# Column sums later on PE, a head split on Vector, 0/1 expert sums in FP32R, and expert weights in 8 KB blocks

## The chip, the cores and the metric

One core of one Trainium2 chip runs the whole program in one launch. The metric is device time in microseconds of one execution. A core has the engines PE (TensorE: matmuls, with weight loads listed as PEld), DVE (VectorE, called Vector here), ACT (ScalarE), POOL (GpSimd) and SP (SyncE, which issues most DMAs). Each engine works through its own instructions in order; semaphores tie them together. Sixteen DMA engines move data between HBM and SBUF.

## The reference

Two transformer blocks on 1024 tokens of width 1024, fp32.

```python
# first block: gated linear attention, then a mixture of experts
x = x + gla_mixer(rmsnorm(x, attn_norm), ...)          # 4 heads, dk 128, dv 256, chunks of 64
h = rmsnorm(x, ffn_norm)
x = rmsnorm(x + hier_moe(h, ...), final_norm)          # 8 groups x 8 experts, top 2 in one group
# an expert: (silu(h @ w1[e]) * (h @ w3[e])) @ w2[e], times the token's gate; summed per token
# second block
mod = silu(c) @ w_ada + b_ada                          # 1 x 1024 by 1024 x 6144, then six parts
...                                                    # SSD + local attention, then a conv FFN
```

w1 and w3 are 1024 x 256 and w2 is 256 x 1024 for each of 64 experts: 3.15 MB an expert, 201 MB in all.

## The kernel before

**First part (phase_gla).** Matmuls of fp32 accuracy are made of three FP32R matmuls: `split_w` (L194) turns a raw weight into a high part (ACT, L135) and a low part (a subtract, L136, on the engine it is given: GpSimd with `G_`, else Vector). For each head, `prep` (L449) projects q, k and two halves of r on PE (`projT`, L309 to L311), yielding after each group of three matmuls. Beside the two r projections it steps `along` (L332), a chain on Vector and ACT that makes the gates and the scaled operands and ends with L391. It also splits the weights needed next; the last, at step 8 of the second r projection, is the second half of the v weight. Then `projV_tile` (L251, L258 to L260) makes v tile by tile, and `core` (L395) does the attention of a head in 128 tokens: matmuls A (L403, L404), a masked copy AT on Vector (L409), matmuls on it (L418 to L421). The code's order is the order on each engine; nothing reorders it.

**Modulation beside it.** `modulation` (L474) is a generator that is stepped by `mod_step` at every second yield of prep(0), prep(1) and prep(2), and at every fourth of head 1's v projection; what is left is drained after prep(2). w_ada comes in 96 chunks of 128 x 512, 12 groups of 8, into six buffers. Vector multiplies each chunk by its scalar and adds it into one of two accumulators (L502, L504). When chunk 1 of the next group has been issued, the group's columns are summed over partitions on PE by `total` (L489): four matmuls of one column (L492), whose result Vector copies to mT at once (L509). At the end mT is turned on PE and stored.

**Expert stage (phase_moe).** Experts are worked through in 32 pairs, expert 2p in PE's columns 0 to 63, expert 2p+1 in 64 to 127; up to 64 slots per expert. Seven weight slots hold w13 (w1 beside w3, 2 MB) and w2 (1 MB) of experts loaded ahead; SP issues a load when the slot's earlier user is done. `load_13` (L920) writes a block of w1 as eight pieces of 1 KB per partition, with w3's pieces between them. A pair on PE, in order of issue:

- `down_t` (L996): the hidden values of the pair before are turned (mhd), Vector copies them (hidT).
- `slots_in` (L1183): the group's tokens are brought into slots by 0/1 matmuls in bf16 (L1189, L1194), ACT copies (xT).
- `rows_out` (L1208): the outputs of two pairs before are brought back to token rows, 160 to a group: y times the gate matrix wT in fp32, rows 0 to 127 in two matmuls of 512 columns (L1220), rows 128 to 159 in four of 256 columns side by side (L1224). ACT copies or Vector adds them (L1216) into Y0 and Y1, which are stored after each fourth pair.
- `hidden` (L980): x times w1 and w3, 16 fp32 matmuls of 512 columns (L986), two at a time; ACT's silu (L990) and Vector's product (L992).
- `turned` (L1199): the gate matrix of the pair is turned (mwt) and copied by ACT. `masks` (L1168): Vector makes the 0/1 and gate matrices of the next pair (L1177 to L1180).
- `down` (L1005): hidden values of the pair before times w2 (L1014), two halves of 512 columns; ACT copies one half to y (tile my), Vector the other (L1016).

Three PSUM buffers (mpy) go round between `down` and `rows_out`. GpSimd issues the gathers of the groups' tokens and the first loads of experts 5 and 6.

Of the kernel before, what the change touches and what calls it, by code (L numbers as in the profile page):

```python
# [70 lines left out]
class Slots:  # L71
# [78 lines left out]
def phase_gla(k, x, attn_norm, w_in, w_gate, b_gate, out_norm, w_o, ffn_norm, w_group, w_expert,  # L150
# [9 lines left out]
    with top:  # L160
# [312 lines left out]

        def modulation():  # L474
# [36 lines left out]
            yield  # L511
            ps = total(11)
# [400 lines left out]
def expert_loads(k, w1, w3, w2):  # L913

    nc = k.nc

    def row(w, e):
        return w[e] if isinstance(e, int) else w[bass.ds(e, 1)].rearrange("o a b -> (o a) b")

    def load_13(e, w, parts=1, eng=(nc.sync, nc.sync)):  # L920
        n = 8 // parts
        for k0 in range(0, 8, n):
            for c, src in enumerate((w1, w3)):
                eng[c].dma_start(out=w[:, k0:k0 + n, c * 256:c * 256 + 256],  # L924
                                 in_=row(src, e).rearrange("(p k) f -> p k f", k=8)[:, k0:k0 + n, :])

    def load_2(e, w, eng=nc.sync):
        eng.dma_start(out=w, in_=row(w2, e).rearrange("(p k) d -> p k d", k=2))

    return load_13, load_2  # L930


def phase_moe(k, h2_d, x1_d, y_d, keep, slots, load_13, load_2, w0):
# [3 lines left out]
    with ExitStack() as ctx:  # L937
# [24 lines left out]

        for name, n in (("my", D), ("MwT", GCAP)):
            sp.tile([128, n], F32, name=name)
        xa, xb = slots.xg, sp.tile([64, D], F32, name="xg1")
# [14 lines left out]
        def hidden(xT, *ws):  # L980
# [3 lines left out]
            for kk in range(8):  # L984
                for c, w in enumerate(ws):
                    nc.tensor.matmul(h[c * 64:c * 64 + 64, :], xT[:, kk, c * 64:c * 64 + 64], w[:, kk, :],  # L986
                                     start=(kk == 0), stop=(kk == 7), skip_group_check=True)

# [15 lines left out]

        def down(hT, *ws):  # L1005

            n = 64 * len(ws)
            y = sp.tile([128, D], F32, name="my")
            for half, copy in ((0, S.copy), (1, V.tensor_copy)):
                cs = slice(half * 512, half * 512 + 512)  # L1010
                ps = pyp.tile([128, 512], F32, name="mpy", tag="mpy")
                for kk in range(2):
                    for c, w in enumerate(ws):
                        nc.tensor.matmul(ps[c * 64:c * 64 + 64, :], hT[:, kk, c * 64:c * 64 + 64], w[:, kk, cs],  # L1014
                                         start=(kk == 0), stop=(kk == 1), skip_group_check=True)
                copy(y[0:n, cs], ps[0:n])  # L1016
                yield y[0:n]

        NP = 32
# [13 lines left out]
        with tc.If(most > GCAP), ExitStack() as over:  # L1033
# [85 lines left out]
            wa, wb = slots.w13(6), slots.w2(6)  # L1119
            x = ov.tile([64, D], F32, name="ox")  # L1120
            V.memset(x, 0.0)
            for j in range(NB):
# [5 lines left out]
                for half in range(2):  # L1128
# [4 lines left out]
                    S.copy(out=xT[:, half * 4:half * 4 + 4, 0:64], in_=ps[:, :, 0:64])  # L1133
                y = list(down(down_t(hidden(xT, wa)), wb))[-1]

# [9 lines left out]
        pb = yp.tile([96, D], BF16, name="xp1")  # L1145
        Y0, Y1 = yp.tile([128, D], F32, name="Y0"), yp.tile([128, 256], F32, name="Y1")

# [14 lines left out]
        def write_group(g):  # L1162
            r = g * GCAP
            for cs in (slice(0, D),) if g < 7 else (slice(0, 512), slice(512, D)):
                S.dma_start(out=y_d[r:r + 128, cs], in_=Y0[:, cs])
            S.dma_start(out=y_d[r + 128:r + GCAP, :].rearrange("t (h c) -> h t c", h=4), in_=Y1)

# [31 lines left out]
        def turned(w):  # L1199
# [43 lines left out]
        for p in range(NP):  # L1243
# [3 lines left out]
            if p > 1:  # L1247
                rows_out(p - 2, wT.pop(p - 2), ys.pop(p - 2))
            if p % 4 == 3 and p // 4 + 1 < 8:
# [11 lines left out]
            if p:  # L1261
                d = down(hT, *pair(w2, p - 1))
                ys[p - 1] = next(d)
# [1386 lines left out]
```

## Time and profile before

| what | us |
|---|---|
| median of 3 runs (lowest, highest) | 2372.03 (2367.1, 2373.81) |
| the profiled execution | 2370.45 |
| its span, first to last instruction | 2368.5 |
| PE busy (share of the span) | 2235.8 (94%) |
| DVE, ACT, POOL busy | 1376.2, 859.9, 569.1 |
| DMA | 408.61 MB, mean 173 GB/s |

Times in the trace are microseconds from the span's start. In the table by stage a row gives the stretch and its length, then the busy microseconds (x instructions) of PE, PEld, DVE, ACT and POOL, then the clock granted to TensorE (1.00 is 2.4 GHz, 0.50 is 1.2 GHz, values between are a mean of the two), the mean busy share of the 16 DMA engines (over 1 where packets overlap), and GB/s. In a timeline a row is one instruction or several alike merged: start, length, engine, line, operation, output<-input, shape, count, and in brackets the idle time before it and what ended it. A PE matmul in fp32 shows as two instructions; a matmul's length includes its way through the array, so the pace is read from start to start.

### The profile page before, as it was taken

What the parts mean: (1) busy time and instruction counts of PE and PEld (TensorE: products, weight loads), DVE (VectorE), ACT (ScalarE), POOL (GpSimd) and SP (SyncE); (2) the same over time, 40 slices, a digit from 0 to 9 for tenths busy, and PEclk for the clock granted to TensorE, in tenths of its full rate; (3) what the DMA queues carried; (4) which work ended last, traced back from release to release, by engine and by line L of the source; (5) the groups of instructions that cost most, each with busy time, mean ns of one, the idle gap of its engine ahead of it and who ended that gap; (6) DMA issues with size and microseconds to landing.
All of it is one profiled execution on the core that took longest, in us unless ns stands there. A gap on an engine that the chain in (4) does not pass through costs nothing.

```text
span 2368.5 us, 31053 instructions
## 1 busy us (share of the span) xinstructions
PE 2235.8 (94%) x11879; PEld 1609.8 (68%) x11879; DVE 1376.2 (58%) x2378; ACT 859.9 (36%) x1610; POOL 569.1 (24%) x520
## 2 busy tenths in 40 slices
PE   8899999996999999998999999999979999999996
PEld 7778888873444444434766788777768888887884
DVE  4766524564443333325355524666588888878988
ACT  4342434311222222214443334424444444444443
POOL 3222223201111111005300100346443333310036
PEclk9999999996999999997999999999989999999999
DMA  5544211648999999997511022444432222227442
GB/s 175 180 123 140 90 33 31 241 179 302 382 395 384 378 374 397 389 395 209 144 39 30 10 43 58 147 99 134 160 98 81 81 81 84 84 91 293 132 138 80
DMA packets 325054, 408.61 MB, mean 173 GB/s; under 512 B 43016, under 2 KB 264312, under 8 KB 316704
## 3 DMA queue, kind: packets, MB, share of 16 engines
q1 hardware_dynamic: 312064, 368.23, 45.9%
q0 software_dynamic: 4944, 18.37, 2.7%
q10 hardware_dynamic: 7888, 19.93, 2.2%
q8 instruction: 96, 1.57, 0.3%
q14 instruction: 62, 0.51, 0.1%
HBM read 360.29 MB, written 46.19 MB: 172 GB/s over the span
## 4 chain that ended last, share of the span: by engine, by line
PE 57%; DVE 5%; DMA 5%; SPq 3%; issue 3%; POOL 2%; ACT 2%; POOLq 0%; DVEq 0%; ACTq 0%
PE mh L986 8%; PE pu L2208 5%; PE pu L2211 5%; PE pu L2210 5%; PE mpy L1014 4%; PE pj L1356 2%; PE pj L1354 2%; PE pj L1352 2%; SPq L924 2%; PE pu L2389 2%; PE mpy L1220 2%; PE pu L2390 2%; PE pu L2387 2%; DMA w<-in_moe_w_dram 2%; PE mtr L1189 1%
## 5 line engine op out<-in xcount | busy, mean ns | idle before, releaser
L986 PE MATMUL mh<-w,xT 128*64 128x512 f32 x880 | 233.4, 598 | 5.7 <-DMA w<-in_moe_w_dram 5.1
L136 POOL TENSOR_TENSOR whl<-wraw,whl 128x1024 fp32r<-128x1024 f32 x35 | 87.1, 2494 | 327.7 <-ACT whl L135 186.5
L986 PEld LDWEIGHTS mh<-w,xT 128*64 128x64 f32 x880 | 76.0, 137 | 123.7 <-issue 108.9
L992 DVE TENSOR_TENSOR hid<-hid,mh 128x256 f32<-128x256 f32 x32 | 13.5, 421 | 220.5 <-ACT hid L990 220.5
L1014 PE MATMUL mpy<-w,hidT 128*64 128x512 f32 x512 | 117.1, 599 | 0.0
L1159 POOL TENSOR_TENSOR xg<-xg,xp 32x1024 f32<-32x1024 f32 x7 | 20.3, 2904 | 372.1 <-ACT xp L1155 372.1
L309 PE MATMUL pj<-hT,whl 128*128 128x512 f32 x256 | 105.4, 412 | 0.7 <-ACT rT L447 0.7
L1356 PE MATMUL pj<-hT,whl 128*128 128x512 f32 x256 | 102.9, 402 | 0.5 <-POOL whl L136 0.5
L1354 PE MATMUL pj<-hT,whl 128*128 128x512 f32 x256 | 103.0, 402 | 0.0
L1352 PE MATMUL pj<-hT,whl 128*128 128x512 f32 x256 | 102.3, 400 | 0.0
L990 ACT ACTIVATE hid<-mh 128x256 f32<-128x256 f32 x32 | 19.8, 619 | 223.9 <-PE mh L986 223.9
L311 PE MATMUL pj<-hT,whl 128*128 128x512 f32 x256 | 100.7, 394 | 0.0
L310 PE MATMUL pj<-hT,whl 128*128 128x512 f32 x256 | 100.5, 393 | 0.0
L2096 POOL TENSOR_TENSOR gr<-wraw,gr 128x512 f32<-128x512 f32 x30 | 58.0, 1932 | 164.2 <-DVE wup L136 59.1
L258 PE MATMUL pj<-whl,hT 128*128 128x256 f32 x256 | 82.5, 322 | 0.6 <-ACT hT L135 0.4
L2217 DVE TENSOR_TENSOR fup<-pu,fup 128x512 f32<-128x512 f32 x100 | 68.6, 686 | 23.0 <-PE pu L2211 23.0
L2389 PE MATMUL pu<-wup 128*128 128x512 f32 x180 | 71.7, 398 | 6.6 <-DVE wup L136 6.6
L259 PE MATMUL pj<-whl,hT 128*128 128x256 f32 x256 | 74.5, 291 | 2.0 <-POOL whl L136 2.0
L260 PE MATMUL pj<-whl,hT 128*128 128x256 f32 x256 | 74.3, 290 | 0.0
L1014 PEld LDWEIGHTS mpy<-w,hidT 128*64 128x64 f32 x512 | 33.8, 136 | 56.1 <-issue 49.1
L504 DVE SCALAR_TENSOR_TENSOR oT<-oT,cv 128x512 f32<-128x512 f32 x84 | 70.5, 839 | 1.4
L2390 PE MATMUL pu<-wup 128*128 128x512 f32 x180 | 70.6, 392 | 0.0
(742 smaller groups left out, 6414.3 us busy)
## 6 DMA issues: line engine op xcount, KB each, us to landing
w<-in_moe_w_dram SPq DMA_DIRECT2D x164, 1024.0 KB
oT<-in_w_ada_dram SPq DMA_DIRECT2D x96, 256.0 KB
wraw<-in_w_up_dram SPq DMA_DIRECT2D x34, 512.0 KB
wraw<-in_moe_w_dram SPq DMA_DIRECT2D x16, 1024.0 KB
wraw<-in_gla_w_in_dram SPq DMA_DIRECT2D x24, 512.0 KB
wraw<-in_w_in_dram SPq DMA_DIRECT2D x22, 512.0 KB
act_d<-act SPq DMA_DIRECT2D x22, 512.0 KB
wraw<-in_w_down_dram SPq DMA_DIRECT2D x42, 256.0 KB
```

Of the source, the lines that this page charges most:

```text
L309: nc.tensor.matmul(ps, w[:, 0, cs], hT[:, 0, kk, sl], start=(kk == 0), stop=False)
L311: nc.tensor.matmul(ps, w[:, 1, cs], hT[:, 0, kk, sl], start=False, stop=(kk == 7))
L986: nc.tensor.matmul(h[c * 64:c * 64 + 64, :], xT[:, kk, c * 64:c * 64 + 64], w[:, kk, :], start=(kk == 0), stop=(kk == 7), skip_group_check ...
L1014: nc.tensor.matmul(ps[c * 64:c * 64 + 64, :], hT[:, kk, c * 64:c * 64 + 64], w[:, kk, cs], start=(kk == 0), stop=(kk == 1), skip_group_che ...
L1352: nc.tensor.matmul(ps, w[:, 0, cs], hT[:, 0, kk, sl], start=(kk == 0), stop=False)
L1354: nc.tensor.matmul(ps, w[:, 0, cs], hT[:, 1, kk, sl], start=False, stop=False)
L1356: nc.tensor.matmul(ps, w[:, 1, cs], hT[:, 0, kk, sl], start=False, stop=(kk == 7))
L2208: nc.tensor.matmul(ps, w[:, 0, cs], hi[:, kk, :], start=(kk == 0 and q in (1, 6, 7, 5)), stop=False, skip_group_check=True)
L2210: nc.tensor.matmul(ps, w[:, 0, cs], lo[:, kk, :], start=False, stop=False, skip_group_check=True)
L2211: nc.tensor.matmul(ps, w[:, 1, cs], hi[:, kk, :], start=False, stop=(kk == 3), skip_group_check=True)
L2389: nc.tensor.matmul(ps, a[:, 0, ts], w[:, 1, :], start=False, stop=False, skip_group_check=True)
L2390: nc.tensor.matmul(ps, a[:, 1, ts], w[:, 0, :], start=False, stop=(kk == 10), skip_group_check=True)
```

## The change

- `modulation`: `total(g - 1)` is issued after chunk 6 of group g, not chunk 1; one more yield stands between it and Vector's copy. Six yields, not two, precede the last total.
- `prep`: for heads 2 and 3 the split at step 8 goes to Vector; for head 1 it stays on GpSimd.
- w13 is laid out as [2, 8, 256], so each of w1 and w3 is one run of 8 KB per partition; `hidden` reads two runs of 256 columns.
- Gates: `turned` makes a 0/1 matrix (Vector, not_equal, FP32R) and the gate of each slot as a row sum (ACT, `accum_out`). `down` scales by the gate and writes y as a high part (ACT, FP32R) and a low part (Vector). `rows_out` multiplies the 0/1 matrix by both parts in FP32R; rows 128 to 159 are now [32, 1024] like the others.
- The overflow path (experts or groups with too many tokens, not taken by these inputs) gets its own `down1`. GpSimd's DMA scratch is set to 8192 bytes.

```diff
@@ Slots.w13
-            return self.raw.rearrange("p a (b c) -> p (a b) c", c=512)
-        return self.tile(i, "w13", [128, 8, 512])
+            return self.raw.rearrange("p (c x) (b f) -> p c (x b) f", c=2, f=256)
+        return self.tile(i, "w13", [128, 2, 8, 256])
@@ prep
-                    st["next"].append(split_w(G_))
+                    st["next"].append(split_w(G_ if h == 1 else None))
@@ modulation
-                if kk == 1 and g > 0:
+                if kk == 6 and g > 0:
                     ps = total(g - 1)
+                    yield
                     V.tensor_copy(mT[:, g * 4 - 4:g * 4], ps[:, 0:4])
-            yield
-            yield
+            for _ in range(6):
+                yield
             ps = total(11)
@@ load_13
-                eng[c].dma_start(out=w[:, k0:k0 + n, c * 256:c * 256 + 256],
+                eng[c].dma_start(out=w[:, c, k0:k0 + n, :],
@@ hidden
-                    nc.tensor.matmul(h[c * 64:c * 64 + 64, :], xT[:, kk, c * 64:c * 64 + 64], w[:, kk, :],
+                    nc.tensor.matmul(h[c * 64:c * 64 + 64, :].rearrange("s (a f) -> s a f", a=2),
+                                     xT[:, kk, c * 64:c * 64 + 64], w[:, :, kk, :], ...
@@ down
-            y = sp.tile([128, D], F32, name="my")
-            for half, copy in ((0, S.copy), (1, V.tensor_copy)):
+            y = sp.tile([128, 2, D], F32R, name="my")
+            for half in range(2):
...
-                copy(y[0:n, cs], ps[0:n])
+                S.activation(out=y[0:n, 0, cs], in_=ps[0:n], func=ACT.Copy, scale=gate)
+                V.scalar_tensor_tensor(out=y[0:n, 1, cs], in0=ps[0:n], scalar=gate, in1=y[0:n, 0, cs].bitcast(F32),
+                                       op0=ALU.mult, op1=ALU.subtract)
@@ turned
-            wT = sp.tile([128, GCAP], F32, name="MwT", bufs=2)
-            S.copy(out=wT, in_=ps)
-            return wT
+            wT = sp.tile([128, GCAP], F32R, name="MwT", bufs=2)
+            gate = sp.tile([128, 1], F32, name="Mgate", bufs=2)
+            junk = sp.tile([128, GCAP], F32, name="Mj")
+            V.tensor_scalar(out=wT, in0=ps, scalar1=0.0, scalar2=None, op0=ALU.not_equal)
+            S.activation(out=junk, in_=ps, func=ACT.Copy, accum_out=gate)
+            return wT, gate
@@ rows_out
-            for half in range(2):
-                cs = slice(half * 512, half * 512 + 512)
-                ps = pyp.tile([128, 512], F32, name="mpy", tag="mpy")
-                nc.tensor.matmul(ps, wT[:, 0:128], y[:, cs], start=True, stop=True)
-                into(Y0[:, cs], ps, (S.copy, V.tensor_copy)[half])
-            ps = pyp.tile([128, 256], F32, name="mpy1", tag="mpy")
-            for i in range(4):
-                nc.tensor.matmul(ps[i * 32:i * 32 + 32], wT[:, 128:GCAP], y[:, i * 256:i * 256 + 256], start=True,
-                                 stop=True, skip_group_check=True)
-            into(Y1, ps, S.copy)
+            for Yn, n, r in ((Y0, 128, 0), (Y1, GCAP - 128, 128)):
+                for half in range(2):
+                    cs = slice(half * 512, half * 512 + 512)
+                    ps = pyp.tile([128, 512], F32, name="mpy", tag="mpy")[0:n]
+                    for i in range(2):
+                        nc.tensor.matmul(ps, wT[:, r:r + n], y[:, i, cs], start=(i == 0), stop=(i == 1))
+                    into(Yn[:, cs], ps, (S.copy, V.tensor_copy)[half])
@@ kernel
-    nc = _bacc.Bacc("TRN2", target_bir_lowering=False, num_devices=1)
+    nc = _bacc.Bacc("TRN2", target_bir_lowering=False, num_devices=1, dynamic_dma_scratch_size=8192)
```

## Rows read from the trace of the kernel before

**Rows 1.** Table by stage; its columns are told in the profile section above.
```profile
60.00:120.00 60.00, 52.94 (x231) 42.12 (x230) 42.15 (x52) 22.94 (x32) 13.78 (x7) 0.91 0.55 173
...
660.00:720.00 60.00, 60.00 (x361) 23.82 (x360) 23.97 (x56) 13.85 (x25) 6.96 (x4) 1.00 1.04 383
```

**Rows 2.** PE's waits: line, releaser, us in total, times, longest.
```profile
PE pj L492 <- DVE oT L504: 12.3, 3, 6.9
...
PE mh L986 <- DMA w<-in_moe_w_dram: 5.1, 3, 2.5
```

**Rows 3.** PE's timeline, one pair: start us, us, line, tiles; count x; [idle before].
```profile
752.35 1.94 PE L1220 MATMUL mpy<-my,MwT 128*128 128x512 f32 x4
...
754.78 7.09 PE L986 MATMUL mh<-w,xT 128*64 128x512 f32 x32
...
770.32 1.08 PE L986 MATMUL mh<-w,xT 128*64 128x512 f32 x4
```

**Rows 4.** PE's timeline, start of the first projection of two late pairs.
```profile
894.58 1.94 PE L986 MATMUL mh<-w,xT 128*64 128x512 f32 x8
...
1060.17 1.08 PE L986 MATMUL mh<-w,xT 128*64 128x512 f32 x4
```

**Rows 5.** PE's timeline, head projection in FP32R, same engine speed.
```profile
90.92 0.39 PE L309 MATMUL pj<-hT,whl 128*128 128x512 f32 x1
...
91.60 0.39 PE L309 MATMUL pj<-hT,whl 128*128 128x512 f32 x1
```

**Rows 6.** Timelines of ACT and DVE, same pair as rows 3.
```profile
748.74 0.58 ACT L1016 COPY my<-mpy 128x512 f32<-128x512 f32 x1 [1.51 <-PE mpy L1014]
...
749.78 0.35 DVE L1180 SCALAR_TENSOR_TENSOR Mw<-Ma,sgate,Mw 128x128 f32<-128x128 bf16 x1
...
750.43 0.69 DVE L1016 COPY my<-mpy 128x512 f32<-128x512 f32 x1 [0.30 <-PE mpy L1014]
```

**Rows 7.** Timelines of PE and DVE around two waits at L492.
```profile
101.34 0.98 PE L492 MATMUL pj<-one,oT 128*128 128x1 f32 x4 [6.86 <-DVE oT L504]
...
111.94 0.27 PE L403 MATMUL A<-D,e 128*128 128x128 f32 x1
...
105.72 4.67 DVE L504 SCALAR_TENSOR_TENSOR oT<-oT,cv 128x512 f32<-128x512 f32 x6
...
112.88 0.30 DVE L409 COPY_PREDICATED AT<-mf,A 128x128 f32<-128x128 int32 x1 [2.49 <-PE A L131]
...
192.94 1.20 PE L492 MATMUL pj<-one,oT 128*128 128x1 f32 x5 [3.98 <-DVE oT L504]
...
195.57 0.29 DVE L409 COPY_PREDICATED AT<-mf,A 128x128 f32<-128x128 int32 x1
```

**Rows 8.** Table by stretch, as rows 1: w1/w3 loads alone, then w2 alone.
```profile
612.00:615.00 3.00, 3.00 (x27) 1.35 (x24) 1.19 (x2) 2.42 (x4) 0.00 (x0) 1.00 1.09 386
...
606.00:608.00 2.00, 2.00 (x12) 0.76 (x10) 0.73 (x3) 0.75 (x2) 0.00 (x0) 1.00 1.01 426
```

**Rows 9.** DMA packets by size in the first stretch of rows 8.
```profile
DMA packets 1153, 1.16 MB, mean 386 GB/s; under 512 B 21, under 2 KB 1153, under 8 KB 1153
```

**Rows 10.** Timelines of DVE and PE at the ends of heads 2 and 3.
```profile
280.34 2.56 DVE L391 SCALAR_TENSOR_TENSOR G<-qk,G 128x1024 f32<-128x1024 f32 x1 [0.79 <-ACT G L384]
...
285.85 0.28 PE L258 MATMUL pj<-whl,hT 128*128 128x256 f32 x1
...
369.18 2.57 DVE L391 SCALAR_TENSOR_TENSOR G<-qk,G 128x1024 f32<-128x1024 f32 x1 [0.78 <-ACT G L384]
...
376.36 0.39 PE L259 MATMUL pj<-whl,hT 128*128 128x256 f32 x1 [2.02 <-POOL whl L136]
```

**Rows 11.** Table by stretch, as rows 1, after three waits of PE.
```profile
97.00:107.20 10.20, 5.86 (x18) 5.02 (x19) 10.16 (x11) 0.58 (x1) 3.64 (x2) 0.50 0.34 104
...
188.80:199.40 10.60, 6.62 (x28) 6.13 (x27) 7.12 (x13) 0.66 (x4) 0.00 (x0) 0.68 0.89 290
...
376.90:380.30 3.40, 3.40 (x18) 3.06 (x16) 0.00 (x0) 0.37 (x1) 0.00 (x0) 0.50 0.50 154
```

More of the change, by code (lines that the diff above doesn't have):

```diff
@@ L961, in phase_moe @@
         get_2(1)
-        for name, n in (("my", D), ("MwT", GCAP)):
-            sp.tile([128, n], F32, name=name)
+        sp.tile([128, 2, D], F32R, name="my")
+        sp.tile([128, GCAP], F32R, name="MwT")
         xa, xb = slots.xg, sp.tile([64, D], F32, name="xg1")
@@ L985, in hidden @@
                 for c, w in enumerate(ws):
-                    nc.tensor.matmul(h[c * 64:c * 64 + 64, :], xT[:, kk, c * 64:c * 64 + 64], w[:, kk, :],
-                                     start=(kk == 0), stop=(kk == 7), skip_group_check=True)
+                    nc.tensor.matmul(h[c * 64:c * 64 + 64, :].rearrange("s (a f) -> s a f", a=2),
+                                     xT[:, kk, c * 64:c * 64 + 64], w[:, :, kk, :], start=(kk == 0), stop=(kk == 7),
+                                     skip_group_check=True)
             hid = sp.tile([128, 2, 128], F32, name="hid")
@@ L1003, in down_t, with down @@
             return hT
-        def down(hT, *ws):
+        def down(hT, gate, *ws):
             n = 64 * len(ws)
-            y = sp.tile([128, D], F32, name="my")
-            for half, copy in ((0, S.copy), (1, V.tensor_copy)):
+            y = sp.tile([128, 2, D], F32R, name="my")
+            for half in range(2):
                 cs = slice(half * 512, half * 512 + 512)
@@ L1015, in down, with down1 @@
                                          start=(kk == 0), stop=(kk == 1), skip_group_check=True)
-                copy(y[0:n, cs], ps[0:n])
+                S.activation(out=y[0:n, 0, cs], in_=ps[0:n], func=ACT.Copy, scale=gate)
+                V.scalar_tensor_tensor(out=y[0:n, 1, cs], in0=ps[0:n], scalar=gate, in1=y[0:n, 0, cs].bitcast(F32),
+                                       op0=ALU.mult, op1=ALU.subtract)
                 yield y[0:n]
+        def down1(hT, w):
+            y = sp.tile([128, 2, D], F32R, name="my").rearrange("p a d -> p (a d)").bitcast(F32)[0:64, 0:D]
+            for half, copy in ((0, S.copy), (1, V.tensor_copy)):
+                cs = slice(half * 512, half * 512 + 512)
+                ps = pyp.tile([128, 512], F32, name="mpy", tag="mpy")
+                for kk in range(2):
+                    nc.tensor.matmul(ps[0:64, :], hT[:, kk, 0:64], w[:, kk, cs], start=(kk == 0), stop=(kk == 1),
+                                     skip_group_check=True)
+                copy(y[:, cs], ps[0:64])
+            return y
         NP = 32
@@ L1119, in phase_moe @@
             wa, wb = slots.w13(6), slots.w2(6)
-            x = ov.tile([64, D], F32, name="ox")
+            x = xb
             V.memset(x, 0.0)
@@ L1133, in phase_moe @@
                     S.copy(out=xT[:, half * 4:half * 4 + 4, 0:64], in_=ps[:, :, 0:64])
-                y = list(down(down_t(hidden(xT, wa)), wb))[-1]
+                y = down1(down_t(hidden(xT, wa)), wb)
                 xo = sp.tile([128, 8, 128], F32, name="oxa", tag="xT")[0:64].rearrange("p a b -> p (a b)")
@@ L1145, in phase_moe @@
         pb = yp.tile([96, D], BF16, name="xp1")
-        Y0, Y1 = yp.tile([128, D], F32, name="Y0"), yp.tile([128, 256], F32, name="Y1")
+        Y0, Y1 = yp.tile([128, D], F32, name="Y0"), yp.tile([GCAP - 128, D], F32, name="Y1")
         def parts(eng=G, cuts=(slice(0, D),)):
@@ L1165, in write_group @@
                 S.dma_start(out=y_d[r:r + 128, cs], in_=Y0[:, cs])
-            S.dma_start(out=y_d[r + 128:r + GCAP, :].rearrange("t (h c) -> h t c", h=4), in_=Y1)
+            S.dma_start(out=y_d[r + 128:r + GCAP, :], in_=Y1)
         def masks(p):
@@ L1216, in into @@
                     V.tensor_tensor(out=out, in0=ps, in1=out, op=ALU.add)
[L1217 to L1226 removed]
+            for Yn, n, r in ((Y0, 128, 0), (Y1, GCAP - 128, 128)):
+                for half in range(2):
+                    cs = slice(half * 512, half * 512 + 512)
+                    ps = pyp.tile([128, 512], F32, name="mpy", tag="mpy")[0:n]
+                    for i in range(2):
+                        nc.tensor.matmul(ps, wT[:, r:r + n], y[:, i, cs], start=(i == 0), stop=(i == 1))
+                    into(Yn[:, cs], ps, (S.copy, V.tensor_copy)[half])
             if p % 4 == 3:
@@ L1247, in phase_moe @@
             if p > 1:
-                rows_out(p - 2, wT.pop(p - 2), ys.pop(p - 2))
+                rows_out(p - 2, wT.pop(p - 2)[0], ys.pop(p - 2))
             if p % 4 == 3 and p // 4 + 1 < 8:
@@ L1261, in phase_moe @@
             if p:
-                d = down(hT, *pair(w2, p - 1))
+                d = down(hT, wT[p - 1][1], *pair(w2, p - 1))
                 ys[p - 1] = next(d)
@@ L1268, in phase_moe @@
                 get_2(*range(*e2[-2:]))
-        rows_out(NP - 2, wT.pop(NP - 2), ys.pop(NP - 2))
-        y = list(down(hT, *pair(w2, NP - 1)))[-1]
-        rows_out(NP - 1, wT.pop(NP - 1), y)
+        rows_out(NP - 2, wT.pop(NP - 2)[0], ys.pop(NP - 2))
+        rows, gate = wT.pop(NP - 1)
+        y = list(down(hT, gate, *pair(w2, NP - 1)))[-1]
+        rows_out(NP - 1, rows, y)
 def pipeline(make, n, every=1, front=False):
```

## The prediction

> **What bounds the kernel now.** I read the table by stage first, then PE's waits, then single stretches of the timelines. The stages show two kinds of work. In the expert stage (some 570 to 1081 us) PE is busy in every microsecond and the DMA engines are at 1.04 of their time with 383 GB/s [rows 1]: two limits lie side by side. In the first part (head projections, with the modulation beside them) PE is short of full, 52.9 of 60 us at a mean clock of 0.91 in 60 to 120 us [rows 1]. PE's waits name two of the causes that the diff touches: 12.3 us at the modulation's column sums (L492) for Vector, and 5.1 us at L986 for expert weights [rows 2]; a third, 2.0 us for a split on GpSimd, comes below. The second block is not touched, and I cost it at nothing.
>
> One pair of experts takes 15.54 us, from one L986 start to the next (754.78, 770.32) [rows 3]. Ten such periods after 894.58 would end at 1049.98; the last pair's L986 starts at 1060.17 [rows 4]. So PE lost 10.2 us there: the 5.1 us of waits, and matmuls that trickle in as pieces land. Until 894 the slower supply only ate into the slots loaded ahead.
>
> **Expert stage, PE.** The part that brings rows back (rows_out) runs from the start of L1220 to the next L986, 752.35 to 754.78, 2.43 us: fp32 matmuls, two of 512 columns and four of 256 side by side [rows 3]. It becomes eight FP32R matmuls of 512 columns. That operation is in the trace: three of them (L309, L310, L311) in 0.68 us, 0.227 each [rows 5], so 8 x 0.227 = 1.82 us. Saved: 0.61 us a pair, in front of L986 of pairs 2 to 31: 30 x 0.61 = 18.3 us, if nothing else gets late. The new period is 14.93 us.
>
> **Expert stage, other engines.** The gates move to y: each half of down is now read by ACT (scaled copy to FP32R), then by Vector (subtract), where one engine read it before. ACT's copy is 0.58 us and ACT idles before it [rows 6]. Vector's subtract I put at 0.78, the six three-operand steps in 4.67 us [rows 7]; bounds 0.69 (its copy of the same tile) [rows 6] and 1.0. Vector also gets a fourth add per pair (up to 0.69) and the 0/1 test of 128x160, 0.3 us by its mask step of 128x128, 0.35 [rows 6]. That is some 1.8 us more a pair on an engine busy 24 of 60 us [rows 1]: hidden as a load. What matters is lateness. Vector ends the masks at 750.13, with the test at 750.43, the two subtracts at 751.2 and 752.0. In this pair PE starts rows_out at 752.35 [rows 3], wants the low part of the first half at 752.58 and of the second at 753.03: margins of 1.4 and 1.0 us. Behind the subtracts on Vector stand only the copy of hidT, which PE wants ten us later, and the adds themselves. The fourth sum reuses the first one's buffer of three 1.37 us after the first began, when its add (0.46 + 0.1 + 0.7) is just over. So nothing per pair; at the very end, where nothing covers it, the added step and the fourth add cost 1.3 us (0.58 + 0.78).
>
> **Expert stage, weights.** w1 and w3 are written in 1 KB pieces (256 values, then a jump); w2 already is 8 KB per partition on both sides, as the new blocks are. The trace has both alone: 386 GB/s over 3 us in which all 1153 packets are under 2 KB [rows 8, 9], and 426 GB/s in a stretch of w2 [rows 8]. A pair needs 4.19 MB of w1/w3 and 2.10 of w2: 4.19/0.386 + 2.10/0.426 = 10.9 + 4.9 = 15.8 us. Where PE waited for weights the period was 165.6/10 = 16.6 [rows 4], so 0.75 us goes to other transfers and gaps. After: 6.29/0.426 + 0.75 = 15.5. Against PE's 15.54 the supply fell behind by 1.0 a pair and took 21 pairs, some 21 us, to empty the slots; against 14.93 it falls behind by 0.6, 17 us in 28 pairs: it just holds. I take back 9 of the 10.2 us. The two edits need each other: with the shorter PE work alone, the supply would set the end. Bounds of the rate: 386 (no gain) and 426. Stage: -18.3 - 9 + 1.3 = -26 us.
>
> A rule of the notes speaks against this part. The Trainium skill (DMA: Bandwidth & Descriptors, Specifications) gives 512 B as the smallest transfer at line rate; by it, 1 KB pieces lose nothing. The 386 beside 426 GB/s disagrees, and I go by the rows.
>
> **Smaller scratch** for GpSimd's own DMAs: it issues few, and the expert weights among them in fewer pieces. Nothing.
>
> **Head split.** In heads 2 and 3 the last v weight goes to Vector. In head 3 PE waited 2.02 us for GpSimd's split at 376.36 [rows 10], then ran at 0.50 clock from 376.9 to 380.3 [rows 11], 1.7 us lost. Vector is free from 369.18 + 2.57 = 371.75 [rows 10]; its split (1.2 for 1024 columns as L391's like, up to 2.6 when slowed as there) ends at 374.3 at the latest, where PE began to wait. -3.5 (0 to -3.7).
>
> **Column sums.** PE no longer stands at L492 for Vector. First wait: 6.86 us before 101.34, then 0.50 clock to 107.2 [rows 7, 11], 2.9 us more. But PE soon wants AT (L409) from Vector. L409 ran at 112.88 after 2.49 us of waiting for PE's A (111.94), yet the six chunk steps from 105.72 to 110.39 stand before it [rows 7]. One tick in nine is now without a chunk, one step less: AT comes at about 109.5, 3.4 us sooner. So I take 3.5 of the 9.8, not all. Second wait: 3.98 us before 192.94, the rest of the 12.3 (1.4) earlier, and a mean clock of 0.68 in 188.8 to 199.4 [rows 7, 11], 3.2 us: 8.6 in all. There Vector has no idle before L409 at 195.57 [rows 7]; two chunk steps and a short wait less before it make 2.3 us, and full speed after it 1.1: 3.4.
>
> Against it: modulation takes 116 yields, not 101, and prep(0) to prep(2) give 113 steps. The last sum, its copy and the turn of mT fall into the drain after prep(2), where PE stands still for Vector. Before, Vector ended head 2's chain at 282.9 and PE went on at 285.85 [rows 10]. Now ten chunk steps (7.8 us) and a split (1.2 to 2.6) enter that chain, whose gaps swallow some 3: it ends at 289 to 290, PE stands 3 to 4 us and may run at half clock after it: +5. Of the moved DMAs, the 96 w_ada loads keep their place behind their chunks on SP, in six buffers, and the store of the modulation is wanted only in the second block. Sums: -3.5 - 3.4 + 5 = -2 us (from -18.4, all waits and slow clock, to +5).
>
> **Sum.** -26 - 3.5 - 2 = -31.5. The profiled execution took 2370.45 us (span 2368.5): 2339. It lies 1.6 below the median of 2372.03; on that, 2340.
>
> **Rivals.**
> (a) Half of the supply gain, 406 GB/s: 6.29/0.406 + 0.75 = 16.2 a pair, 1.3 behind PE; the slots are empty after some 17 pairs and twelve pairs pay, 15 us of waits in place of 1: 2354. For it: the mix of pieces gives 383 over 60 us [rows 1]. Chance 0.15.
> (b) The supply stays at 16.6 a pair, as if 1 KB pieces lost nothing: the last weights land when they did, PE's 18.3 us become waits at L986. Left are the first part (-5.5) and the tail (+1.3): 2368. Against it: rows 8. Chance 0.06. (This is what the Trainium skill's 512 B line would make of it.)
> (c) The column sums give all back: PE has work wherever Vector is late, and the drain costs nothing. -26 - 3.5 - 18.4 = -48: 2324. Against it: Vector is full up to both L409 [rows 7]. Chance 0.12.
> (d) Slower: the second reading of down. If Vector's subtracts come later than the margin of 1 us, PE stands at the FP32R matmuls of every pair. To undo 31.5 us takes 1.05 us a pair, a lateness of 2.1 us; at 3.5 us it is 30 x 2.5 - 31.5 = +43: 2415. Against it: Vector keeps up with the end of down, idle 0.30 before its copy [rows 6]. Chance 0.05.
> The forecast itself has 0.62, own range 2332 to 2350.
>
> **Chances.** A change under 0.3% (7 us) can't be told from none. Faster: forecast, (a) and (c), 0.89; same: (b), 0.06; slower: (d), 0.05. The range leaves out half of (c), (b) and (d): 2325 to 2359.
>
> **What would show it.** L1220 to L986 at 1.8 us, a pair at 14.9; 8 KB packets and 410 GB/s or more; no wait for weights over 1 us before the last pairs. In the first part no wait of several us at L492 before head 2's end, but waits at the matmuls on AT and one at the turn of mT. Wrong would be: PE waiting for my in each pair, or a rate under 400.

## The result and the profile after

The changed kernel takes 2349.89 us (median of 4 runs, 2348.68 to 2351.78), against 2371.76 (4 runs, 2367.1 to 2373.81) for the kernel before on the same chip: a ratio of 0.9911, 95% interval 0.9894 to 0.9928. It is 21.9 us faster; I had forecast 31.5. The profiled execution took 2348.68 us with a span of 2346.7, before 2370.45 and 2368.5 [time and profile before].

Where the 21.8 us of the two profiled executions lie, by the starts of the first w1 matmul of pairs 0, 1 and 31 (570.0, 583.8 and 1060.2 before; 568.1, 582.4 and 1038.2 after): 1.9 ahead of the expert stage, -0.5 in the first pair, 20.6 in the thirty pairs behind it (476.4 against 455.8), -0.5 in the tail, 0.3 in the second block, which the change doesn't touch.

PE's timeline of the same pair as [rows 3], in the changed kernel:

```profile
762.62 2.14 PE L1241 MATMUL mpy<-my,MwT 128*128 128x512 f32 x8
764.69 7.09 PE L987 MATMUL mh<-w,xT 128*64 128x512 f32 x32
...
777.77 2.33 PE L1241 MATMUL mpy<-my,MwT 128*128 128x512 f32 x8
780.02 0.65 PE L987 MATMUL mh<-w,xT 128*64 128x512 f32 x2
```

The eight FP32R matmuls of rows_out now stand for 764.69 - 762.62 = 2.07 us ahead of the next w1 matmul, where six fp32 ones stood for 2.43. A pair takes 15.13 to 15.15; every fourth, in which a group of tokens starts, 15.33 (here 780.02 - 764.69). Before it was 15.53.

The table by stage, columns as in [rows 1]: the stretch from pair 1 to pair 31, one slice with the limits of [rows 1], and the last third of the pairs.

```profile
582.40:1038.20 455.80, 455.44 (x2762) 198.10 (x2762) 230.77 (x507) 141.40 (x255) 51.37 (x31) 1.00 0.98 402
660.00:720.00 60.00, 59.96 (x368) 26.00 (x364) 31.18 (x68) 19.00 (x34) 7.29 (x4) 1.00 0.95 391
...
900.00:1030.00 130.00, 129.88 (x774) 55.11 (x773) 63.69 (x138) 39.48 (x71) 12.90 (x7) 1.00 1.01 424
```

PE is busy in 455.44 of 455.80 us, and from pair 2 on no pair takes more than 15.33: PE alone sets the end there. The 5.1 us of waits for weights [rows 2] are gone, and with them the matmuls that trickled in as pieces landed. In the last third the loads run at 424 GB/s, about the rate that only w2 had before (426) [rows 8]. Vector is busy 31.2 of 60 us (24.0 before), and PE doesn't wait for it.

PE's waits in the changed kernel (as [rows 2]; the 12.3 us at L492 have become the first line), and its timeline and Vector's around the longest of them (as [rows 7]):

```profile
PE OD L418 <- ACT ks L412: 12.4, 4, 6.5
...
PE pj L492 <- DVE oT L504: 1.3, 1, 1.3
PE pj L131 <- DVE mT L514: 1.2, 1, 1.2
...
PE pj L259 <- DVE whl L136: 0.8, 1, 0.8
...
PE mpy L1241 <- DVE my L1019: 0.6, 2, 0.3
```

```profile
110.89 1.22 PE L418 MATMUL OD<-vt,ks 128*128 128x256 f32 x2 [6.48 <-ACT ks L412]
...
103.83 2.57 DVE L502 TENSOR_SCALAR oT<-oT,cv 128x512 f32<-128x512 f32 x1
106.43 3.90 DVE L504 SCALAR_TENSOR_TENSOR oT<-oT,cv 128x512 f32<-128x512 f32 x5
110.25 0.29 DVE L409 COPY_PREDICATED AT<-mf,A 128x128 f32<-128x128 int32 x1
```

PE no longer stands at the column sums, but for 1.3 us at the last one. It stands at L418 instead, for ACT's copies L412 and L413, which wait for Vector's L409, which stands behind six chunk steps (one L502, five L504). The wait is 6.48 us where it was 6.86 [rows 7].

### The profile page after: what moved, and what is told of

The parts are those of the page before. It is cut to its first block, busy times and chain, and to the rows that moved or that the text cites. A ratio compares the mean times of both kernels' runs of the same rounds, so it can differ in the third digit from the quotient of the medians.

```text
span 2346.7 us, 30954 instructions
## 1 busy us (share of the span) xinstructions
PE 2219.3 (95%) x11751; PEld 1608.4 (69%) x11751; DVE 1437.1 (61%) x2476; ACT 894.5 (38%) x1674; POOL 565.5 (24%) x518
## 4 chain that ended last, share of the span: by engine, by line
PE 62%; DVE 5%; issue 2%; DMA 2%; ACT 2%; POOL 2%; SPq 0%; POOLq 0%; ACTq 0%; DVEq 0%
PE mh L987 10%; PE pu L2225 5%; PE pu L2228 5%; PE pu L2227 5%; PE mpy L1016 5%; PE mpy L1241 2%; PE pj L1373 2%; PE pj L1371 2%; PE pj L1369 2%; PE pu L2406 2%; PE pu L2407 2%; PE pu L2404 2%; PE mtr L1205 2%; PE ctr L1612 1%; PE ctr L131 1%
## 5 line engine op out<-in xcount | busy, mean ns | idle before, releaser
L987 PE MATMUL mh<-w,xT 128*64 128x512 f32 x880 | 229.4, 599 | 0.6 <-ACT xT L1212 0.5
L987 PEld LDWEIGHTS mh<-w,xT 128*64 128x64 f32 x880 | 71.4, 137 | 120.4 <-issue 118.4
L2234 DVE TENSOR_TENSOR fup<-pu,fup 128x512 f32<-128x512 f32 x100 | 68.6, 686 | 21.9 <-PE pu L2228 21.9
L504 DVE SCALAR_TENSOR_TENSOR oT<-oT,cv 128x512 f32<-128x512 f32 x84 | 75.0, 893 | 4.4 <-DMA oT<-in_w_ada_dram 3.1
L2406 PE MATMUL pu<-wup 128*128 128x512 f32 x180 | 71.6, 398 | 6.2 <-DVE wup L136 6.2
L259 PE MATMUL pj<-whl,hT 128*128 128x256 f32 x256 | 74.1, 290 | 0.8 <-DVE whl L136 0.8
L1241 PE MATMUL mpy<-my,MwT 128*128 128x512 f32 (+1 forms) x256 | 70.6, 408 | 1.2 <-DVE my L1019 0.6
## 6 DMA issues: line engine op xcount, KB each, us to landing
wraw<-in_moe_w_dram SPq DMA_DIRECT2D x16, 1024.0 KB, 15.5
```

What stands on the lines that cost most here:

```text
L987: nc.tensor.matmul(h[c * 64:c * 64 + 64, :].rearrange("s (a f) -> s a f", a=2), xT[:, kk, c * 64:c * 64 + 64], w[:, :, kk, :], start=(kk = ...
L1241: nc.tensor.matmul(ps, wT[:, r:r + n], y[:, i, cs], start=(i == 0), stop=(i == 1))
L2406: nc.tensor.matmul(ps, a[:, 0, ts], w[:, 1, :], start=False, stop=False, skip_group_check=True)
```

## The experiments

Each run's ratio is to the kernel before, measured beside it on the same chip (medians of before 2370.87 to 2373.88); what is said in us compares medians, and less than 3 us is within the spread of these. Code is cut at "...". Runs 1 to 4 take back one part of the change each.

**Run 1: w1 and w3 in 1 KB pieces again.**

```diff
-        return self.tile(i, "w13", [128, 2, 8, 256])
+        return self.tile(i, "w13", [128, 8, 512])
-                eng[c].dma_start(out=w[:, c, k0:k0 + n, :],
+                eng[c].dma_start(out=w[:, k0:k0 + n, c * 256:c * 256 + 256],
...
```

> The changed kernel with w1 and w3 written in 1 KB pieces again; all else as changed. Theory (the piece size sets the supply, and two thirds of the gain hang on it): the supply goes back to some 16.6 us a pair, PE's shorter pairs (15.13 instead of 15.53) turn into waits for weights, the last pairs start their w1 matmuls at about 1059 us as before, and the time is 2368 to 2372 us, 20 above the changed kernel's 2349.9; in the waits some 15 to 20 us of PE's matmuls on w13 for DMA. Rival (1 KB pieces lose nothing, the 386 GB/s had another cause): no wait for weights, 2350. Between, 2357 to 2363, if only the old starvation of 10 us comes back.

Measured: 2365.97 us (ratio 0.9974, 0.9964 to 0.9983), so 16.1 slower than the changed kernel. Of its trace, the line for the w1 matmuls among PE's waits (us in total, times, longest):

```profile
PE mh L987 <- DMA w<-in_moe_w_dram: 7.0, 6, 1.7
```

The table's rows of an early and a late stretch:

```profile
600.00:660.00 60.00, 59.96 (x366) 26.00 (x364) 31.22 (x68) 19.00 (x34) 7.24 (x4) 1.00 1.06 395
900.00:1050.00 150.00, 143.90 (x828) 65.38 (x826) 67.79 (x150) 41.95 (x77) 12.88 (x7) 1.00 1.06 395
```

PE's timeline at the starts of pairs 20 and 31:

```profile
871.77 1.07 PE L987 MATMUL mh<-w,xT 128*64 128x512 f32 x2
...
1055.85 1.94 PE L987 MATMUL mh<-w,xT 128*64 128x512 f32 x8
```

Up to 871.8 the pairs keep the new pace; from there eleven take (1055.85 - 871.77)/11 = 16.73 us each. With 1 KB pieces the loads run at 395 GB/s at a DMA share of 1.06, and that sets the end. The time is 2 us under the theory's range, and the waits come to 7.0 us, not 15 to 20: the rest of the 17 us that these pairs lose is w1 and w3 matmuls that trickle in (7.15 us from the first start to the last in the pair at 922.72, which has no wait, and 6.50 in an undisturbed one). The rival in which the piece costs nothing falls, and so does the prediction's rival (b): its 2368 is about what the change gives without this edit.

**Run 2: rows brought back as before** (fp32, gates in the masks), 8 KB pieces kept.

```diff
-                    for i in range(2):
-                        nc.tensor.matmul(ps, wT[:, r:r + n], y[:, i, cs], start=(i == 0), stop=(i == 1))
+                nc.tensor.matmul(ps, wT[:, 0:128], y[:, cs], start=True, stop=True)
...
```

> The kernel before with the 8 KB weight blocks, the new column sums, the head split and the small scratch, but with down and the bringing back of rows as before (fp32, gates in the masks). Theory (PE's own work sets the end once the weights come in 8 KB pieces): a pair takes 15.53 again, 0.39 x 30 = 11.7 us more than the changed kernel, less 0.5 at the tail: 2361, with no wait for weights. Rival (the transfers set the pair at 15.13 too, and the 0/1 sums gain nothing): 2350. Second rival (the starvation stays): 2370.

Measured: 2359.53 (0.9950, 0.9935 to 0.9964), 9.6 slower than the changed kernel. PE's timeline at the starts of pairs 1 and 31:

```profile
582.21 1.15 PE L987 MATMUL mh<-w,xT 128*64 128x512 f32 x4 [0.51 <-ACT xT L1198]
...
1049.44 1.24 PE L987 MATMUL mh<-w,xT 128*64 128x512 f32 x4
```

467.2 us for thirty pairs, 15.57 each: PE's old pace to the end but for one pair that takes 16.7, in which a w1 matmul waits for weights; so the old starvation goes with the piece size alone. In this stage the 0/1 sums are worth 467.2 - 455.8 = 11.4 us (1.2 of it that one pair), in the time 9.6.

**Run 3: the column sums two chunks behind Vector again.**

```diff
-                if kk == 6 and g > 0:
+                if kk == 1 and g > 0:
                     ps = total(g - 1)
-                    yield
-            for _ in range(6):
-                yield
+            yield
+            yield
```

> The changed kernel with the column sums of modulation issued two chunks behind Vector again, all else as changed. Theory (the waits at the column sums only moved to the matmul on AT and into the drain): the time stays within 3 us of 2349.9, and the first expert pair starts within 3 us of 568.1; waits of 12 us at the column sums in place of 12 at the matmul on AT. My forecast's term: 2 us slower, 2352. Rival (the column sums were a full gain of 18 us that other parts of the change gave back): 2368.

Measured: 2348.13 (0.9902, 0.9887 to 0.9917), 1.8 less than with the edit, with overlapping intervals. "PE pj L492" is back at 12.2 us in its profile and L418 is gone from the list; pair 0 starts at 567.0. The edit gains nothing; whether it costs the 1.8 us is not shown. My term of 2 us faster does not come out, and the rival of 18 us is refuted by far.

**Run 4: the last v weight of heads 2 and 3 split on GpSimd again.**

```diff
-                    st["next"].append(split_w(G_ if h == 1 else None))
+                    st["next"].append(split_w(G_))
```

> The changed kernel with the last v weight of heads 2 and 3 split on GpSimd again, all else as changed. Theory: head 3 waits 2 us for the split and runs at half clock for 3.4 us behind it, 3.5 us together: 2353.4, with head 3's end later by 3.5. Rival (PE's clock falls and its wait comes at other places anyway, the edit is worth nothing): 2350.

Measured: 2353.08 (0.9923, 0.9910 to 0.9937), 3.2 slower, with overlapping intervals, so that the trace has to carry the cause. The wait of head 3 is back among PE's waits:

```profile
PE pj L259 <- POOL whl L136: 2.0, 1, 2.0
```

And with it the dip of the clock, to a mean of 0.88 in the table's row of that stretch:

```profile
376.00:390.00 14.00, 11.98 (x78) 11.10 (x77) 1.61 (x5) 3.56 (x9) 5.48 (x4) 0.88 0.25 76
```

The theory had only head 3. In head 2, too, the split on GpSimd (281.79, 2.83 us) costs time, because it runs beside a step of Vector that takes 1.21 us in the changed kernel:

```profile
282.30 3.40 DVE L383 SCALAR_TENSOR_TENSOR D<-qk,D 128x1024 f32<-128x1024 f32 x1
```

The last column sum then waits 3.5 us for Vector instead of 1.3. From head 3's first v matmul to its last L421 this run takes 49.5 us, as the kernel before does, and the changed kernel 46.8: head 3's part is 2.7 us, not 3.5.

**Run 5: what bounds the expert stage now.** The low half of y is left out of rows_out.

```diff
-                    for i in range(2):
-                        nc.tensor.matmul(ps, wT[:, r:r + n], y[:, i, cs], start=(i == 0), stop=(i == 1))
+                    nc.tensor.matmul(ps, wT[:, r:r + n], y[:, 0, cs], start=True, stop=True)
```

> The changed kernel with only the high half of y in the bringing back of rows (four matmuls instead of eight; the low half is left out): PE has 4 x 0.235 = 0.94 us less a pair, a pair of 14.2. It asks what bounds the stage now. Theory (my figure of the supply, 15.5 a pair with 8 KB pieces): the supply falls behind by 1.3 a pair, the slots filled ahead cover 20 us of 39, and 19 of PE's 28 us come back as waits for weights at the w1 matmuls: 2341, pairs of 15.5 in the last third. Rival (PE alone sets the end, the supply has room, the mean of 402 GB/s being what PE asks for): no such wait, 2322.

Measured: 2341.01 (0.9875, 0.9860 to 0.9890). The time hits the theory's number, but not by its sum. In the trace the fourth sum of rows_out waits for the buffer of the first, whose add has only begun; the waits for the adds and copies of Y come to 11.5 us, so a pair takes 14.68 and 15.10 in every fourth, not 14.2. The timelines of PE and DVE in one pair, and then PE's waits:

```profile
699.72 0.94 PE L1240 MATMUL mpy<-my,MwT 128*128 128x512 f32 x3
...
700.24 1.88 DVE L1235 TENSOR_TENSOR Y<-mpy,Y 128x512 f32<-128x512 f32 x3 [0.63 <-PE mpy L1240]
...
701.33 0.65 PE L987 MATMUL mh<-w,xT 128*64 128x512 f32 x2
```

```profile
PE mpy L1240 <- DVE Y L1235: 6.3, 20, 0.3
PE mpy L1240 <- ACT Y L1233: 5.2, 7, 0.7
```

The starts of pairs 22 and 31 in PE's timeline, and the table's row between them:

```profile
893.87 1.07 PE L987 MATMUL mh<-wraw,xT 128*64 128x512 f32 x2
...
1032.54 1.94 PE L987 MATMUL mh<-w,xT 128*64 128x512 f32 x8
```

```profile
894.00:1030.00 136.00, 132.41 (x771) 60.28 (x771) 66.80 (x149) 40.12 (x73) 13.15 (x9) 1.00 1.01 424
```

The other half of the theory holds: from 893.87 on nine pairs take 15.41 us each, while the DMA engines move 424 GB/s at a share of 1.01. The longer pairs are longer in their w1 and w3 matmuls (7.40 us from the first start to the last in the pair at 893.87, 6.50 in an undisturbed one); the 3.6 us in which PE idles in this row are the waits for Y, as before. That is the supply with 8 KB pieces; I had put it at 15.5. At the changed kernel's 15.19 a pair it lies 0.2 behind PE, and the slots cover that.

**Runs 6, 7, 10, 11 and 12: Vector's backlog in heads 0 to 2.** Run 6 moves modulation's steps to where Vector has room:

```diff
+        early = True
-        for _ in prep(0, wq):
-            mod_step(2)
+        for i in prep(0, wq):
+            n = next(ticks)
+            early = early and i != "qk"
+            if n % 4 if early else n % 4 == 0:
+                next(mod, None)
...
-                    mod_step(2)
+                    mod_step(2 if early or h == 2 else 4)
...
-                    if h == 1:
-                        mod_step(4)
+                    if h == 1 and t > 0:
+                        mod_step(2)
```

> The changed kernel with modulation's steps put elsewhere: in head 0 three of four ticks while q and k are projected and one of four beside the gates, in head 1 one of four beside the gates, and one of two instead of one of four beside head 1's v; the same 96 chunk steps. Theory (PE's waits of 6.5 and 5.3 us at the matmul on AT come from the chunk steps that stand on Vector before L409, and the drain from the yields that are left): both waits shrink to 2 us or less, the drain and the turn of mT go, the first expert pair starts 8 to 14 us earlier than 568.1, and the time is 2337 to 2343. Rival (Vector is full in these heads whatever the order; the wait goes to the next matmul that needs Vector): 2347 to 2352.

Measured: 2338.54 (0.9865, 0.9850 to 0.9880), 11.4 faster than the changed kernel; pair 0 starts at 555.8, 12.3 earlier. The wait of 5.3 us is gone (2.85 for a split on GpSimd are new, at 179), the one at 104 is left with 4.8 us, where the theory said 2 or less. PE's busy time and clock between 60 and 290 us, in the changed kernel's table rows and then in this run's:

```profile
60.00:120.00 60.00, 53.52 (x230) 42.72 (x229) 39.99 (x48) 23.11 (x32) 14.35 (x7) 0.91 0.50 162
120.00:290.00 170.00, 159.86 (x832) 132.50 (x831) 112.32 (x175) 63.36 (x132) 40.57 (x41) 0.96 0.41 125
```

```profile
60.00:290.00 230.00, 219.02 (x1154) 180.80 (x1153) 155.85 (x232) 91.31 (x179) 65.38 (x53) 0.99 0.44 137
```

5.6 us more of work, and the clock at 0.99: the waits cost twice, as lateness and as half clock behind them. So what counts in these heads is that Vector isn't behind, not how far behind it PE issues the sums. Run 11 says so directly: run 6 with the sums two chunks behind again (the edit of run 3).

> The kernel with modulation's steps put elsewhere (2338.5), but with the column sums two chunks behind Vector, as before, and two empty yields at the end. Theory (what counts is that Vector isn't behind; with the steps put elsewhere the distance of the sums matters little): within 3 us of 2338.5. Rival (the seven chunks' distance carries the gain there): 8 us or more slower, waits at the column sums.

Measured: 2337.88 (0.9858, 0.9842 to 0.9874), the same as run 6 and the fastest here.

Run 7 gives the first chunk step of each sum to ACT:

```diff
-                    V.tensor_scalar(out=acc, in0=w, scalar1=cv[:, 0:1], scalar2=None, op0=ALU.mult)
+                    S.activation(out=acc, in_=w, func=ACT.Copy, scale=cv[:, 0:1])
```

> The changed kernel with the first of the eight chunk steps of each sum on ACT (a scaled copy) in place of Vector: twelve steps of 0.7 to 2.6 us less on Vector. Theory (Vector's backlog sets the waits at the matmul on AT): each of the two waits shrinks by 2 to 3 us, 2344 to 2346. Rival (ACT, in order, makes the step late, or the backlog is elsewhere): 2350 or slower.

Measured: 2349.11 (0.9904, 0.9891 to 0.9918): nothing, the rival's side. The first wait fell from 6.5 to 6.0, the second stayed at 5.3. Vector's timeline before the two L409 shows why:

```profile
105.25 5.99 DVE L504 SCALAR_TENSOR_TENSOR oT<-oT,cv 128x512 f32<-128x512 f32 x5
...
191.56 1.54 DVE L504 SCALAR_TENSOR_TENSOR oT<-oT,cv 128x512 f32<-128x512 f32 x2 [0.95 <-DMA oT<-in_w_ada_dram]
```

Before the first, GpSimd's split (104.61, 2.93 us) now runs beside the steps that are left: five take 5.99 us where five took 3.90. Before the second, Vector itself stands 0.95 us for a load of w_ada.

Run 10 takes GpSimd's splits beside the gates, and GL, to Vector in run 6's kernel:

```diff
-            G_.tensor_tensor(out=GL, in0=GL, in1=kk, op=ALU.mult)
+            V.tensor_tensor(out=GL, in0=GL, in1=kk, op=ALU.mult)
...
-            wr1 = split_w(G_)
+            wr1 = split_w()
...
```

> The kernel with modulation's steps put elsewhere (2338.5), and in each head the splits beside the gates and the product GL on Vector instead of GpSimd. In that run's trace a chunk step of 0.75 us takes 2.83 to 2.90 where GpSimd's subtract or product runs beside it. Theory (GpSimd's operation costs Vector some 2.1 us, doing it on Vector costs 1.2): Vector's backlog gets shorter, the 4.8 us before the matmul on AT at 104 and the 2.85 us for the split at 179 shrink, 2331 to 2335. Rival (a split on Vector waits there for ACT's cast and holds all behind it): 2339 to 2346.

Measured: 2343.09 (0.9883, 0.9868 to 0.9898), 4.6 slower than run 6, in the rival's range. The wait at 104 stayed at 4.8 us, the turn of mT waits 2.9, and PE waits 3.5 us in two places for splits on Vector (L259). That those splits wait for ACT's cast, as the rival has it, is not shown.

Run 12 puts all of head 0's steps ahead of its gates, in run 11's kernel:

```diff
-            if n % 4 if early else n % 4 == 0:
+            if early and n % 8:
```

> The last kernel (steps put elsewhere, sums two chunks behind, 2337.9) with head 0's steps all ahead of its gates: seven of eight ticks while q and k are projected, none beside the gates. Theory (the wait of 4.8 us at 105 is the three or four chunk steps that stand on Vector before the first L409): it shrinks to 1.5 us or less and the half clock behind it goes, 2332 to 2336. Rival (the gates alone fill Vector there, or the faster steps wait for their loads): 2337 to 2341.

Measured: 2340.81 (0.9868, 0.9851 to 0.9884), not faster than run 11. The wait at 105 is gone, as the theory said, but PE now waits 1.1 and 2.2 us at L492 (62 and 70 us), 3.2 for a split on GpSimd and 3.4 at the turn of mT: the rival.

**Runs 8 and 9: pieces of 2 KB.** Run 8 by four transfers an expert and tensor instead of one:

```diff
-                load_13(e, w13[e], 2 if e in (7, 8, 63) else 1, **kw)
+                load_13(e, w13[e], 4, **kw)
```

> The changed kernel with w1 and w3 loaded in four transfers each, so that a piece is 2 KB instead of 8 KB; bytes and places are the same. Theory (a cost per piece: 386 GB/s at 1 KB and 426 at 8 KB give 408 at 2 KB, so the supply takes 4.19/0.408 + 4.92 + 0.75 = 15.95 a pair, 0.8 behind PE's 15.13): the slots cover most of it, 2 to 8 us of waits for weights in the last pairs, 2352 to 2358. Rival (from 2 KB on a piece is free): 2350. Rival (eight transfers an expert are held up at their issue on SP): over 2366, slower than 1 KB in two transfers.

Measured: 2437.42 (1.0288, 1.0261 to 1.0316), far over the 2 KB theory, and 71 over 1 KB pieces in whole transfers; the rival of the eight transfers has the time right. The table's row of this run, and then the line of its waits of SP's queue, and the changed kernel's:

```profile
800.00:1100.00 300.00, 270.46 (x1445) 115.02 (x1446) 125.84 (x272) 75.23 (x135) 27.47 (x15) 0.97 0.96 334
```

```profile
SPq L925 <- DMA w<-in_moe_w_dram: 223.6, 290, 4.5
```

```profile
SPq L925 <- DMA w<-in_moe_w_dram: 111.1, 53, 4.5
```

SP stands at 290 issues instead of 53 for earlier loads, and the rate falls to 334 GB/s. That SP's waits are the cause is not shown: the DMA engines' share is still 0.96. Run 9 keeps one transfer and changes the layout, so that only the piece differs:

```diff
-        return self.tile(i, "w13", [128, 2, 8, 256])
+        return self.tile(i, "w13", [128, 4, 2, 2, 256])
...
-                                 in_=row(src, e).rearrange("(p k) f -> p k f", k=8)[:, k0:k0 + n, :])
+                                 in_=row(src, e).rearrange("(p q k) f -> p q k f", q=4, k=2)[:, k0 // 2:(k0 + n) // 2])
...
```

> The changed kernel with w1 and w3 laid out so that a piece is 2 KB, in two transfers an expert as in the changed kernel: the piece size alone, without the eight transfers of the run before. Theory (a cost per piece, 408 GB/s at 2 KB from 386 at 1 KB and 426 at 8 KB): the supply takes some 15.9 a pair, 0.7 behind PE; the slots filled ahead, worth 13 us by the run with the high half alone, last some 19 pairs: 4 to 9 us of longer pairs at the end, 2353 to 2359. Rival (from 2 KB on a piece costs nothing): 2350. Rival (the eight transfers were not the cause, pieces of 2 KB are slow): over 2400.

Measured: 2354.90 (0.9928, 0.9914 to 0.9942), in the theory's range. The row of its last pairs:

```profile
900.00:1040.00 140.00, 138.40 (x810) 64.59 (x809) 66.52 (x147) 41.65 (x76) 12.89 (x7) 1.00 1.04 411
```

395, 411 and 424 GB/s at 1, 2 and 8 KB: a cost per piece. The packets of w1 and w3 show it directly: between 900 and 1030 us the median one takes 46 ns at 1 KB (run 1), 84 at 2 KB (run 9) and 309 at 8 KB (changed kernel, w2's among them), that is some 8.4 ns a packet and 27 bytes a ns besides. One transfer cut into four costs far more than a piece of 2 KB. In run 8 the median packet takes 84 ns too, but the mean 98 against 85 in run 9, and the engines' share there is 0.97 against 1.04. Run 8 also reads HBM in runs of 2 KB, where run 9 reads 8 KB; no run separates the two.

## Why the prediction was right, and where not

The mechanism of the main part was right, its first term too large, and one small part gained nothing.

- **The FP32R sums** (I put -18.3): the step that failed, by size. I took 8 x 0.227 = 1.82 us from a run of FP32R matmuls that follow one another [rows 5]; it took 2.07. Two more starts of that rows_out, from the changed kernel's timeline of PE, show where the 0.25 lies:

```profile
762.93 0.39 PE L1241 MATMUL mpy<-my,MwT 128*128 128x512 f32 x1
...
764.37 0.40 PE L1241 MATMUL mpy<-my,MwT 128*32 128x512 f32 x1
```

  With 762.62 and 764.69 from above: the first matmul is followed after 0.31 us, the last one, by the fp32 w1 matmul, after 0.32, and the six between take 0.24 each. So some 0.18 lies at the two ends, where the kind of matmul changes, and the rest is spread over the six. In the head projection it is the same: after the turn of GL (L131) its first matmul is followed 0.31 us later, against 0.227 in the run.

```profile
102.69 0.33 PE L131 MATMUL A<-ident,GL 128*128 128x128 f32 x1
102.78 0.47 PE L309 MATMUL pj<-hT,whl 128*128 128x512 f32 x1
103.09 0.39 PE L310 MATMUL pj<-hT,whl 128*128 128x512 f32 x1
```

  That the change of kind is the reason is my reading; no run separates it. A second step failed, by less: I put the reuse of the first sum's buffer at nothing. In every fourth pair ACT copies that sum, behind its two copies of xT, and the fourth sum waits for it:

```profile
778.78 1.22 ACT L1233 COPY Y<-mpy 128x512 f32<-128x512 f32 x2
...
779.44 0.14 PEld L1241 LDWEIGHTS mpy<-my,MwT 128*32 128x32 f32 x2 [0.56 <-ACT Y L1233]
```

  With 0.39 saved a pair, and 0.2 given back in seven of them, thirty pairs give 10.3 us instead of 18.3; run 2 has 11.4 in the stage and 9.6 in the time.
- **The weights** (-9 of 10.2): right; all of the starvation went, the other 10.3 of the 20.6 us (run 2). Rival (a), a supply at 406 GB/s, fell with it: 424, and no wait. That the two edits need each other is shown: the 8 KB pieces are worth 16.1 us with the shorter sums (run 1), the sums 9.6 with the 8 KB pieces (run 2), and both together 21.9 - 3.2 + 1.8 = 20.5, not 25.7. So alone they would give 20.5 - 9.6 = 10.9 and 20.5 - 16.1 = 4.4. The new supply of 15.5 a pair was 15.41 (run 5). The rule of the Trainium skill (DMA: Bandwidth & Descriptors, Specifications) that 512 B reaches line rate is contradicted by runs 1 and 9, at 1 and at 2 KB (395 and 411 GB/s against 424).
- **Vector's lateness, rival (d)**: didn't come. PE waited 0.6 us in all for the subtracts, at the last pairs; the margins of 1.4 and 1.0 us held.
- **The smaller scratch** (nothing): no run takes it back by itself.
- **The tail** (+1.3): +0.5 from pair 31's start to the second block's.
- **The head split** (-3.5): 3.2 (run 4). That the numbers lie so close is partly luck: head 3, where I put all of it, gives 2.7, and run 4 also loses time in head 2, where GpSimd's split slows Vector beside it. Vector's split ran from 373.49 to 376.91, slower than the 2.6 that I allowed, so PE still waited 0.8; the clock did not dip.
- **The column sums** (-2, from -3.5, -3.4 and +5): no gain, +1.8 in the medians (run 3); rival (c), -18.4, fell. L409 came at 110.25, 2.6 earlier than before (I had 109.5), the second at 191.83, 3.7 earlier in all, so the second term gave 1.1 instead of 3.4: the full speed that I counted behind it didn't come. The clock was half behind L418 as it had been behind L492 (0.50 in 109.2 to 116.0, 0.51 in 191 to 198). The drain took it all back: head 2's first v matmul behind it starts at 286.33, against 285.85 [rows 10]. Run 3, which differs in the sums alone, shows it best. The last projection of head 2 and the first v matmul, in the changed kernel and then in run 3:

```profile
282.32 0.39 PE L311 MATMUL pj<-hT,whl 128*128 128x512 f32 x1
...
286.33 0.36 PE L258 MATMUL pj<-whl,hT 128*128 128x256 f32 x1
```

```profile
286.55 0.39 PE L311 MATMUL pj<-hT,whl 128*128 128x512 f32 x1
286.78 0.28 PE L258 MATMUL pj<-whl,hT 128*128 128x256 f32 x1
```

  PE comes to the drain 4.2 us earlier and leaves it 0.45 earlier, with a mean clock of 0.79 from 282 to 290 where run 3 has 1.00; head 3's first v matmul then starts at 374.4 against 373.3.

So -26 became -20.1 in the thirty pairs and the tail, -3.5 came out at -2.7 in head 3, and -2 became nothing or a small loss. The signs that I named came out as follows: L1241 to L987 2.07, not 1.8; a pair 15.14, not 14.9; the pieces at 424 GB/s (at least 410 was said); no wait for weights at all; the wait at the matmuls on AT and the one at the turn of mT, as said. One caution on the first part: it is the same code in the changed kernel and in runs 1, 2, 5, 8 and 9, and pair 0 starts there anywhere from 568.1 to 570.4 us; the 1.9 us of the single profile are within that.

## What to carry to other kernels

Where two limits lie side by side, price both sides per period: here shorter matmuls and larger DMA pieces each paid only as far as the other let them. A wait of PE for an engine with a backlog isn't removed by issuing the waiting instruction later, since the next one that needs that engine stands behind the same backlog; move the backlog to where the engine has room. And take the price of a matmul from a row with the same neighbours, not from the middle of a long run of its kind.

## What the runs showed of the hardware

A chunk step of Vector that takes 0.75 us takes 2.90 beside a GpSimd operation of 3.27 us. Vector's and GpSimd's timelines in run 6:

```profile
95.89 2.90 DVE L504 SCALAR_TENSOR_TENSOR oT<-oT,cv 128x512 f32<-128x512 f32 x1
98.71 2.88 DVE L386 SCALAR_TENSOR_TENSOR Ex<-qk,Ex 128x512 f32<-128x512 f32 x1
...
108.58 0.74 DVE L504 SCALAR_TENSOR_TENSOR oT<-oT,cv 128x512 f32<-128x512 f32 x1
```

```profile
94.97 3.27 POOL L136 TENSOR_TENSOR whl<-wraw,whl 128x1024 fp32r<-128x1024 f32 x1 [14.41 <-ACT whl L135]
98.19 2.85 POOL L390 TENSOR_TENSOR GL<-GL,qk 128x1024 f32<-128x1024 f32 x1
```

The Trainium skill (SBUF — State Buffer, Who interferes with whom) says that a Vector instruction with two inputs in SBUF contends with a GpSimd instruction that reads SBUF, for a port pair that is locked to one of them at a time. The trace agrees: both Vector steps end 0.55 us behind GpSimd's (98.79 behind 98.24, 101.59 behind 101.04), 2.90 and 2.88 us long. Yet moving those GpSimd operations to Vector lost 4.6 us (run 10). Two more sizes I had not expected: pieces still matter above 1 KB (395, 411 and 424 GB/s at 1, 2 and 8 KB; 46, 84 and 309 ns a packet), and four transfers in place of one take the rate of 2 KB pieces from 411 to 334 GB/s, for a reason that is open.
